# One transformer kernel with its instruction order redrawn: new prices in the planner, and engines chosen by it

## The chip, the cores and the metric

The kernel runs on one core of one Trainium2 chip. The metric is the device time of one execution in microseconds, here the median of three runs. The core has five engines that run side by side: TensorE (PE, with its weight loads as PEld), VectorE (DVE), ScalarE (ACT), GpSimd (POOL) and SyncE (SP), which in this kernel only issues DMAs.

## The reference

Two layers of a diffusion backbone in float32, on 512 latent tokens and 256 context tokens of 1024 features. Each layer is a token mixer and a squared-ReLU MLP, both on normalised input that a vector `c` shifts, scales and gates (adaLN).

```python
for i in range(DEPTH):                     # DEPTH = 2
    mod_lat = (silu_c @ ada_w[i] + ada_b[i])[:, None, :]
    mod_ctx = (silu_cc @ ada_w[i] + ada_b[i])[None, None, :]
    u_lat = modulate(rms_norm(h_lat, g_mix[i]), sh1, sc1)
    u_ctx = modulate(rms_norm(h_ctx, g_mix[i]), csh1, csc1)
    # layer 0: 16 heads, 2-D neighbourhood attention with a bias table, plus all context keys
    # layer 1: 16 query heads on 4 key heads, window of 128, rotary embedding, a sink logit
    h_lat = h_lat + ga1 * y_lat
    h_lat = h_lat + ga2 * squared_relu_mlp(modulate(rms_norm(h_lat, g_mlp[i]), sh2, sc2), mlp_w1[i], mlp_w2[i])
    # layer 0 does the same for the context rows; layer 1 does not need them
```

## The kernel before

Large products are made exact enough by splitting: each operand becomes a rounded part and a rest (`split`, line 581: a copy on ACT, a subtraction on DVE or POOL), and three products stand for one. Activations are kept as features by tokens in `FA`, split operands in `RA`, both cut by hand into rings of slots.

In order of time the stages are: the start (modulation of the first layer, first QKV, `ada01`, `mods01`, `mod0`); the first attention (`qkv0`, `attn0`, from about 90 us); output projection and entry of the first MLP (about 400 to 500 us); the first MLP in 16 chunks with the second layer's modulation made on ACT and POOL beside it (`ada`, to 1045 us); keys, values and queries of the second layer (`kv1`); the second attention (`Head1`, to about 1290 us); the second MLP on latent tokens only.

The order of the instructions isn't the order of the code. Calls on engines only record steps. `Plan` knows which step needs which, gives each step a cost (`cost`, line 206), and plays the program through its own model of the five engines (`forward`, line 276): at each time the engine that is free first takes the ready step with the lowest rank. `search` repeats this 40 times with other ranks, keeps the shortest, and the steps are then issued engine by engine in that order (line 432, to which the profile puts nearly all instructions). SP's queue is a part of the plan, so loads are reordered too. The engine of a step is fixed in the code: `v`, `s`, `g` stand for DVE, ACT, POOL.

Names that matter below: `load` (line 559) issues a DMA from SP; `bias_tables` (line 780) copies 32 pieces of the relative bias into a table in DRAM, from which every head of the first attention reads (`attn0`, line 933); `ada_ring`, `raw` and `w0` are the rings that loads of the start wait for; `Stats.step` sums squares for a norm; `dup_mult` (line 816) scales queries and keys by their norms; `evac_pt` (line 919) and `merge` (line 925) bring attention results out of PSUM; in `attn0` and `Head1.front` the probabilities are multiplied by the reciprocal of their sum, on DVE for most blocks and on POOL for one in four; `Stream.fill` loads and splits weights, with POOL as the subtracting engine around the entries of the MLPs (`stream.eng = g`) and DVE in their bodies.

Of the kernel before, what the change touches and what calls it, by code (L numbers as in the profile page):

```python
# [10 lines left out]
F32 = mybir.dt.float32  # L11
# [8 lines left out]
L = 512  # L20
# [68 lines left out]
class Step:  # L89


    def __init__(self, eng):
        self.eng, self.calls, self.reads, self.writes = eng, [], [], []
        self.epoch, self.deps, self.succ = None, set(), []
        self.occ = self.dur = 0.0
        self.mode, self.port, self.bytes = "R", False, 0.0

# [18 lines left out]
class Plan:  # L116
    LANES = {"tensor": "PE", "vector": "DVE", "scalar": "ACT", "gpsimd": "POOL", "sync": "SP"}
    ALL = ("PE", "DVE", "ACT", "POOL", "SP")
    WINDOW = 3413.3

# [35 lines left out]
    def add(self, step):  # L156
# [4 lines left out]
        for x, write in [(x, False) for x in step.reads] + [(x, True) for x in step.writes]:  # L161
# [9 lines left out]
            for k in self.cells(x):  # L171
# [3 lines left out]
                if write:  # L175
                    d.update(r)
                elif kind == "PSUM":

                    d.update(j for j in r if self.steps[j].eng != step.eng)
# [9 lines left out]
        d.discard(i)  # L189
        self.cost(step)  # L190
# [15 lines left out]
    def cost(self, x):  # L206
        if x.eng == "PE":
# [9 lines left out]
            if kind == "t":  # L217
                x.occ, x.dur = 109.0, 272.0
# [22 lines left out]
        else:  # L241
            f, args, kw = x.calls[0]
            data = [(y, *width(y)) for y in x.reads]
            n = max(width(y)[0] for y in x.reads + x.writes)
            here = [(y, m) for y, _, m in data if self.space(y) == "SBUF" and m > 8]
            psum = any(self.space(y) == "PSUM" for y in x.reads)
            if x.eng == "ACT":
                two = f == "activation" and len(data) > 1
                x.dur = (165 + 0.81 * n if psum else 195 + 0.83 * n) + (95 if two else 0) + (90 if kw.get("accum_out") is not None else 0)
                if n <= 8:  # L250
                    x.dur = 297.0 if two else 205.0
                x.occ = x.dur - 105
            elif x.eng == "DVE":
                x.dur = 148 + 1.045 * n
                if len(data) > 2:
                    x.dur += 62
                if n <= 16:
                    x.dur = 157.0
                elif f == "tensor_scalar" and not psum:
                    x.dur = 225 + 0.51 * n  # L260
                x.occ = x.dur - 82 + (82 if kw.get("accum_out") is not None else 0)
                x.port = f not in ("tensor_reduce", "reciprocal", "memset") and not psum and (len(here) > 1 or f in ("tensor_scalar", "tensor_copy") or n <= 8)
            else:
                wide = any(m < k for _, k, m in data)
                x.dur = 470 + 2.33 * n if f == "tensor_scalar" else 80 + 0.8 * n if f in ("memset", "affine_select") else 170 + (1.75 if wide else 2.2) * n
                x.occ = x.dur - 45
                x.port = f not in ("memset", "affine_select")

    LAG = {"PE": 54.0, "POOL": 80.0, "SP": 60.0, "DVE": 35.0, "ACT": 35.0}
# [6 lines left out]
    def forward(self, rank):  # L276

        L = self.steps
        n = len(L)
        wait = [len(x.deps) for x in L]  # L280
# [5 lines left out]
        for x in L:  # L286
            if not x.deps:
                heapq.heappush(coming[x.eng], (0.0, rank[x.i], x.i))
        for _ in range(n):
            t, e = min((max(free[e], min(([free[e]] if now[e] else []) + ([coming[e][0][0]] if coming[e] else []))), k, e) for k, e in enumerate(self.ALL) if now[e] or coming[e])[::2]  # L290
            while coming[e] and coming[e][0][0] <= t + 1e-6:
                _, k, i = heapq.heappop(coming[e])
                heapq.heappush(now[e], (k, i))
            k, i = heapq.heappop(now[e])
            x = L[i]
            if e == "PE" and x.mode != mode and now[e]:

                later = [(k, i)]
                while now[e] and now[e][0][0] < k + 250:
                    y = heapq.heappop(now[e])  # L300
                    if L[y[1]].mode == mode:
# [11 lines left out]
            if e == "PE":  # L313
# [5 lines left out]
                pre = 0.0 if x.mode == mode else 95.0 if mode == "R" else 100.0  # L319
# [12 lines left out]
            elif e == "SP":  # L332
                free[e] = t + x.occ
                dma = max(t + 1500, dma) + x.bytes
                end[i] = dma + 800
            else:
                hold = max(0.0, port - t) if x.port else 0.0
                free[e] = t + hold + x.occ
# [1457 lines left out]
```

## Time and profile before

| | us |
|---|---|
| median of three runs | 1660.36 (1658.4 to 1661.73) |
| profiled execution | 1661.9 |
| its span, first to last instruction | 1660.1 |
| PE busy in it | 1601.2 |
| mean granted clock of TensorE | 0.992 |

The profile is of one execution. Busy time of an engine is the time in which it has at least one instruction under way; products overlap in PE, so a busy PE need not be a well-fed one. A stage is a stretch of the span. The granted clock is the share of full speed that TensorE was given; it has two levels, 1.2 and 2.4 GHz. A wait belongs to what ended last before the waiting instruction could start.

### The profile page before, as it was taken

What the parts mean: (1) busy time and instruction counts of PE and PEld (TensorE: products, weight loads), DVE (VectorE), ACT (ScalarE), POOL (GpSimd) and SP (SyncE); (2) the same over time, 40 slices, a digit from 0 to 9 for tenths busy, and PEclk for the clock granted to TensorE, in tenths of its full rate; (3) what the DMA queues carried; (4) which work ended last, traced back from release to release, by engine and by line L of the source; (5) the groups of instructions that cost most, each with busy time, mean ns of one, the idle gap of its engine ahead of it and who ended that gap; (6) DMA issues with size and microseconds to landing.
All of it is one profiled execution on the core that took longest, in us unless ns stands there. A gap on an engine that the chain in (4) does not pass through costs nothing.

```text
span 1660.1 us, 25159 instructions
## 1 busy us (share of the span) xinstructions
PE 1601.2 (96%) x9554; PEld 1357.5 (82%) x9554; DVE 1136.5 (68%) x2178; ACT 808.7 (49%) x1668; POOL 553.9 (33%) x371
## 2 busy tenths in 40 slices
PE   4999999999989999999999999999999899999999
PEld 3878888987778888888888888797767888888887
DVE  4787666778458656675666666899996766655654
ACT  4587666778435334344352433658874522332320
POOL 1121111122247419485682652475631400000000
PEclk9999999999999999999999999999999899999999
DMA  9723443114314334334342332010114232233301
GB/s 295 213 74 102 134 150 121 47 42 126 103 63 128 97 101 132 103 114 127 115 140 76 115 106 73 32 58 14 46 45 146 89 102 90 89 101 102 102 26 52
DMA packets 63802, 165.63 MB, mean 100 GB/s; under 512 B 6848, under 2 KB 24640, under 8 KB 63552
## 3 DMA queue, kind: packets, MB, share of 16 engines
q1 hardware_dynamic: 63680, 164.02, 31.2%
q8 instruction: 75, 1.23, 0.3%
q14 instruction: 47, 0.39, 0.1%
HBM read 159.79 MB, written 7.34 MB: 101 GB/s over the span
## 4 chain that ended last, share of the span: by engine, by line
PE 80%; DVE 8%; ACT 5%; issue 3%; DMA 3%; POOL 1%; SPq 0%; POOLq 0%; DVEq 0%; ACTq 0%
PE pq L432 80%; DVE FA L432 3%; DVE RA L432 2%; ACT RA L432 2%; DVE smalls L432 1%; DMA FA<-in_ada_w_dram 1%; ACT FA L432 1%; ACT R L432 1%; DMA FA<-in_wqkv_dram 1%; POOL FA L432 0%; DVE R L432 0%; ACT smalls L432 0%; DMA R<-in_ada_w_dram 0%; SPq L432 0%; DMA FA<-in_wo_dram 0%
## 5 line engine op out<-in xcount | busy, mean ns | idle before, releaser
L432 PE MATMUL pq<-RA 128*128 128x512 f32 (+3 forms) x6784 | 1268.5, 342 | 13.1 <-DVE RA L432 5.4
L432 PEld LDWEIGHTS pq<-RA 128*128 128x128 f32 x6784 | 1083.1, 190 | 166.8 <-issue 16.6
L432 ACT CAST RA<-FA 128x1024 fp32r<-128x1024 f32 (+3 forms) x283 | 224.9, 812 | 370.7 <-PE pq L432 256.5
L432 DVE TENSOR_TENSOR RA<-FA,RA 128x1024 fp32r<-128x1024 f32 (+3 forms) x249 | 297.5, 1209 | 113.6 <-ACT RA L432 109.9
L432 DVE SCALAR_TENSOR_TENSOR FA<-pq,mods,FA 128x512 f32<-128x512 f32 (+1 forms) x413 | 266.0, 662 | 138.6 <-PE pq L432 137.4
L432 POOL TENSOR_TENSOR R<-R,FA 128x1024 f32<-128x1024 f32 x84 | 218.2, 2628 | 6.7 <-ACT FA L432 4.6
L432 POOL TENSOR_TENSOR FA<-FA,smalls 128x512 f32<-128x512 f32 (+1 forms) x108 | 95.9, 892 | 322.5 <-DVE smalls L432 250.4
L432 PE MATMUL pq<-RA,R 128*128 128x512 f32 (+1 forms) x870 | 177.6, 353 | 3.4 <-DVE RA L432 3.4
L432 PEld LDWEIGHTS pq<-RA,R 128*128 128x128 f32 x870 | 144.4, 191 | 27.6 <-DVE RA L432 3.8
L432 POOL TENSOR_SCALAR FA<-FA,s 128x1024 f32<-128x1024 f32 x24 | 77.5, 3230 | 180.8 <-DMA FA<-in_ada_w_dram 166.0
L432 PE MATMUL pq<-ident,FA 128*128 128x128 f32 x802 | 124.1, 276 | 9.4 <-DVE FA L432 2.5
L432 PEld LDWEIGHTS pq<-ident,FA 128*128 128x128 f32 x802 | 92.0, 140 | 30.4 <-issue 9.4
L432 POOL TENSOR_TENSOR FA<-FA 128x256 f32<-128x256 f32 (+2 forms) x97 | 75.2, 791 | 120.2 <-ACT FA L432 109.4
L432 POOL TENSOR_TENSOR RA<-FA,RA 128x1024 fp32r<-128x1024 f32 (+2 forms) x34 | 72.4, 2140 | 128.5 <-ACT RA L432 96.4
L432 ACT COPY R<-pq 128x512 f32<-128x512 f32 (+3 forms) x200 | 89.6, 477 | 37.6 <-PE pq L432 36.4
L432 ACT ACTIVATE FA<-FA,smalls 128x512 f32<-128x512 f32 (+1 forms) x120 | 89.1, 743 | 25.4 <-DVE smalls L432 25.0
L432 ACT COPY FA<-pq 128x256 f32<-128x256 f32 (+4 forms) x130 | 56.1, 432 | 87.5 <-PE pq L432 80.1
L432 ACT ACTIVATE FA<-FA,s 128x1024 f32<-128x1024 f32 x60 | 69.1, 1151 | 60.1 <-POOL FA L432 50.8
L432 DVE SCALAR_TENSOR_TENSOR FA<-pq,FA 128x512 f32<-128x512 f32 (+1 forms) x96 | 57.1, 596 | 53.5 <-ACT FA L432 53.4
L432 ACT ACTIVATE FA<-pq 128x512 f32<-128x512 f32 (+1 forms) x96 | 49.9, 522 | 73.0 <-PE pq L432 71.9
L432 ACT ACTIVATE FA<-FA 128x256 f32<-128x256 f32 (+1 forms) x131 | 59.0, 457 | 49.5 <-DVE FA L432 38.3
L432 PE MATMUL pq<-R 128*64 128x512 f32 (+2 forms) x448 | 78.9, 463 | 0.0
(77 smaller groups left out, 979.1 us busy)
## 6 DMA issues: line engine op xcount, KB each, us to landing
FA<-in_w_dram SPq DMA_DIRECT2D x128, 512.0 KB, 3.5
FA<-in_ada_w_dram SPq DMA_DIRECT2D x80, 512.0 KB, 3.9
FA<-in_wqkv_dram SPq DMA_DIRECT2D x32, 384.0 KB, 3.7
FA<-in_wo_dram SPq DMA_DIRECT2D x16, 512.0 KB, 3.5
FA<-in_ada_w_dram SPq DMA_DIRECT2D x20, 256.0 KB, 5.9
FA<-in_wq_dram SPq DMA_DIRECT2D x8, 512.0 KB, 3.6
R<-in_ada_w_dram SPq DMA_DIRECT2D x12, 256.0 KB, 6.3
FA<-in_xT_dram SPq DMA_DIRECT2D x4, 512.0 KB, 7.7
```

The costliest lines, as they stand in the source:

```text
L432: tc.keep_in_program_order(getattr(e, f)(*map(real, args), **{k: real(x) for k, x in kw.items()}))
```

## The change

Three things change, all of them in how the plan is drawn.

First, the planner's prices. Each instruction on DVE, ACT and POOL is planned 40 ns longer than its price (`SPARE`). PE's turning between kinds of product has a table (`TURN`) in place of one number, DMAs are planned to land 2000 instead of 800 ns after their bytes, POOL's answer takes 110 instead of 80 ns, a change of the partitions that an engine starts at costs it a drain, and DVE and POOL hold each other off where both need the port that they share.

Second, steps with several forms. `gv` is "POOL or DVE", `sv` "ACT or DVE", and `scaled` "POOL, DVE or ACT", each with POOL or ACT first in the list. Such a step waits in the queues of all its engines. The first engine of the list gives it up when another would end it earlier by more than the step's slack and 50 ns; another engine takes it early only when its slack is small. Weight splits, sums of squares, norm scalings, rope products, PSUM copies, and the scaling of probabilities become such steps.

Third, loads made through `load` before the first attention are issued in program order (`strict`). That puts the bias tables' copies behind the loads of the first modulation and QKV weights, among the loads of the next QKV weights.

```diff
+    SPARE = 40.0
...
+            forms = x.forms or {x.eng: x.calls[0]}
+            for e, c in forms.items():
+                occ, dur, port = self.vector_cost(x, e, *c)
+                x.costs[e] = occ + self.SPARE, dur + self.SPARE, port
+            x.occ, x.dur, x.port = x.costs[x.eng]
...
+    TURN = {("t", "R"): -81.0, ("R", 64): 92.0, ("R", 32): 90.0, ("t", 64): 93.0, ("t", 32): 93.0,
+            (64, "R"): 62.0, (64, "t"): 62.0, (32, "R"): 137.0, (32, "t"): 137.0, (32, 64): 112.0, (64, 32): 112.0, (64, 64): -38.0, (32, 32): 22.0}
+    DRAIN = {"DVE": 113.0, "ACT": 127.0, "POOL": 0.0}
-    LAG = {"PE": 54.0, "POOL": 80.0, "SP": 60.0, "DVE": 35.0, "ACT": 35.0}
+    LAG = {"PE": 54.0, "POOL": 110.0, "SP": 60.0, "DVE": 35.0, "ACT": 35.0}
...
+            if e == "POOL" and owner == "DVE" and port > t + 150 and L[now[e][0][1]].costs[e][2]:
+                free[e] = port - 65
+                continue
...
+            if x.forms:
+                own, slack = x.costs[e][1], k - t
+                if e == x.eng:
+                    best = min(max(free[o], t) + c[1] for o, c in x.costs.items())
+                    if free_choice and t + own > best + max(50.0, slack):
+                        dropped.add(i)
+                        continue
+                elif i not in dropped:
+                    main = max(free[x.eng], t) + x.costs[x.eng][1]
+                    if not free_choice or slack > main - t + 200 or main <= t + own:
+                        heapq.heappush(coming[e], (t + 300, k, i))
+                        continue
+                gone[i] = True
+                eng[i] = e
...
-                pre = 0.0 if x.mode == mode else 95.0 if mode == "R" else 100.0
+                pre = self.TURN.get((mode, x.mode), 0.0)
...
-                end[i] = dma + 800
+                end[i] = dma + 2000
...
-                hold = max(0.0, port - t) if x.port else 0.0
+                hold = max(0.0, port - t - 138) if shared and owner != e else 0.0
+                if low[e] != x.low or not x.low and e == "DVE":
+                    hold += self.DRAIN[e]
...
+    gv, sv = Engine("gpsimd", "vector"), Engine("scalar", "vector")
+    def scaled(out, x, by, flat):
+        y = Step("POOL")
+        y.forms = {"POOL": ("tensor_tensor", (), dict(out=out, in0=x, in1=by, op=ALU.mult)),
+                   "DVE": ("tensor_scalar", (), dict(out=out, in0=x, scalar1=flat, scalar2=None, op0=ALU.mult)),
+                   "ACT": ("activation", (out, x, AF.Copy), dict(scale=flat))}
+        y.calls, y.reads, y.writes = [y.forms["POOL"]], [x, by], [out]
+        plan.add(y)
...
-    load = sy.dma_start
+    strict = [True]
+    def load(out, in_):
+        x = sy.dma_start(out, in_)
+        if strict[0]:
+            if strict[1:]:
+                x.after = strict.pop().i
+                x.deps.add(x.after)
+            strict.append(x)
...
     def split(H_, L_, x, eng=None):
         s.copy(H_, x)
-        (eng or v).tensor_tensor(out=L_, in0=x, in1=H_.bitcast(F32), op=ALU.subtract)
+        gv.tensor_tensor(out=L_, in0=x, in1=H_.bitcast(F32), op=ALU.subtract)
...
-                g.tensor_tensor(out=acc[0], in0=acc[0], in1=tmp, op=ALU.add)
+                gv.tensor_tensor(out=acc[0], in0=acc[0], in1=tmp, op=ALU.add)
...
                 s.activation(q, h, AF.Square)
-                eng.tensor_tensor(out=R, in0=R, in1=q, op=ALU.add)
+                gv.tensor_tensor(out=R, in0=R, in1=q, op=ALU.add)
...
-        (v.tensor_copy if eng is v else s.copy)(pt[:, 0 : hi - lo], ps[:, lo:hi])
+        sv.copy(pt[:, 0 : hi - lo], ps[:, lo:hi])
...
-            if t == 0:
-                g.tensor_tensor(out=P, in0=P, in1=sm.broadcast_to([128, 512]), op=ALU.mult)
-            else:
-                v.tensor_scalar(out=P, in0=P, scalar1=sm, scalar2=None, op0=ALU.mult)
+            scaled(P, P, sm.broadcast_to([128, 512]), sm)
...
     weave((qk, 6), (bias_tables(), 16))
+    strict[0] = False
...
-            v.tensor_tensor(out=hL, in0=q, in1=hH.bitcast(F32), op=ALU.subtract)
+            gv.tensor_tensor(out=hL, in0=q, in1=hH.bitcast(F32), op=ALU.subtract)
...
-            g.tensor_tensor(out=h4(y), in0=h4(x), in1=rope[:, 2 * e, t].unsqueeze(1).broadcast_to([128, 4, DH]), op=ALU.mult)
+            gv.tensor_tensor(out=h4(y), in0=h4(x), in1=rope[:, 2 * e, t].unsqueeze(1).broadcast_to([128, 4, DH]), op=ALU.mult)
```

Copies out of PSUM in `merge`, the fronts of the projections and the values become `sv`; the remaining products of `roped` and `dup_mult` become `gv`; the scalings of `Head1.front` become `scaled` in the same way as those shown.

## Rows read from the trace of the kernel before

**Rows 1.** The page, part 1: busy us, share of span, instructions.

```profile
PE 1601.2 (96%) x9554; PEld 1357.5 (82%) x9554; DVE 1136.5 (68%) x2178; ACT 808.7 (49%) x1668; POOL 553.9 (33%) x371
```

**Rows 2.** Stages: length, busy PE, PEld, DVE, ACT, POOL; granted clock, DMA share, GB/s.

```profile
20.00:100.00 80.00, 70.03 (x585) 60.15 (x577) 58.06 (x148) 46.17 (x125) 17.03 (x22) 0.96 0.66 200
100.00:470.00 370.00, 362.89 (x2433) 310.72 (x2432) 247.77 (x719) 249.64 (x677) 74.96 (x82) 1.00 0.31 99
470.00:501.00 31.00, 24.62 (x133) 21.02 (x132) 20.88 (x30) 14.98 (x25) 16.18 (x8) 0.83 0.22 68
501.00:1045.00 544.00, 544.00 (x3140) 472.95 (x3140) 369.18 (x487) 217.86 (x299) 312.49 (x126) 1.00 0.35 110
1045.00:1095.00 50.00, 46.15 (x278) 39.26 (x277) 44.88 (x85) 29.59 (x64) 25.66 (x31) 1.00 0.09 27
1095.00:1300.00 205.00, 199.28 (x1390) 158.51 (x1390) 178.35 (x432) 142.29 (x333) 89.31 (x91) 0.99 0.19 61
1300.00:1320.00 20.00, 16.59 (x109) 15.73 (x108) 13.03 (x20) 9.69 (x17) 10.30 (x5) 0.83 0.34 106
1320.00:1660.00 340.00, 336.75 (x1489) 278.32 (x1487) 198.62 (x245) 90.87 (x118) 7.31 (x3) 1.00 0.26 84
```

**Rows 3.** Chain of waits, shares by line: 501 to 1045, 1095 to 1310 us.

```profile
by line: PE pq L432 100.0%
...
by line: PE pq L432 67.8%; DVE FA L432 14.5%; issue 4.1%; DVE R L432 3.0%; ACT FA L432 3.0%; DVE RA L432 2.6%; DVE smalls L432 1.7%; ACT R L432 1.7%; ACT RA L432 1.5%; ACT smalls L432 0.4%; DVEq L432 0.0%; ACTq L432 0.0%
```

**Rows 4.** Timeline of SP's queue and PE: start, us, instructions, wait before.

```profile
8.59 0.34 SPq L432 DMA_DIRECT2D cst<-in_cst_dram  x1
...
20.27 5.17 SPq L432 DMA_DIRECT2D bias_e<-in_rpb_dram  x7
...
57.32 1.01 SPq L432 DMA_DIRECT2D FA<-in_wqkv_dram  x2
...
19.06 1.94 PE L432 MATMUL pq<-FA,s 128*32 128x128 f32 x32 [19.06 <-DVE s L432]
...
57.56 10.50 PE L432 MATMUL pq<-RA 128*128 128x384 f32 x59
...
91.56 3.29 PE L432 MATMUL pq<-RA 128*128 128x256 f32 x20 [0.42 <-DVE smalls L432]
```

**Rows 5.** Timeline, all engines, entry of the first MLP.

```profile
478.99 10.56 POOL L432 TENSOR_TENSOR RA<-FA,RA 128x1024 fp32r<-128x1024 f32 x3 [6.45 <-ACT RA L432]
...
479.64 0.74 DVE L432 SCALAR_TENSOR_TENSOR FA<-FA,amod 128x512 f32<-128x512 f32 x1
...
479.91 8.35 PE L432 MATMUL pq<-RA 128*128 128x512 f32 x36
...
484.83 2.48 DVE L432 SCALAR_TENSOR_TENSOR FA<-FA,amod 128x512 f32<-128x512 f32 x1
...
494.64 1.22 PE L432 MATMUL pq<-FA,ones 128*128 128x256 f32 x2 [6.38 <-POOL FA L432]
...
495.30 5.25 PE L432 MATMUL pq<-RA 128*128 128x512 f32 x11
```

**Rows 6.** Groups: busy us, mean ns, idle; second attention (three), first, whole span.

```profile
L432 DVE TENSOR_SCALAR FA<-FA,smalls 128x640 f32<-128x640 f32 x24 | 20.1, 865 | 0.0
...
L432 DVE TENSOR_SCALAR FA<-FA,smalls 128x512 f32<-128x512 f32 x16 | 12.5, 780 | 0.1
...
L432 POOL TENSOR_TENSOR FA<-FA,smalls 128x512 f32<-128x512 f32 x28 | 31.3, 1124 | 44.6 <-DVE smalls L432 31.6 <-ACT R L432 7.5 <-ACT FA L432 5.4
...
L432 DVE TENSOR_SCALAR FA<-FA,smalls 128x512 f32<-128x512 f32 x39 | 18.7, 492 | 0.1
...
L432 POOL TENSOR_TENSOR RA<-FA,RA 128x1024 fp32r<-128x1024 f32 x19 | 50.1, 2646 | 60.0 <-ACT RA L432 36.1 <-PE pq L432 21.4 <-DVE RA L432 2.5
```

**Rows 7.** Timeline, entry of the second MLP.

```profile
1308.20 2.56 DVE L432 SCALAR_TENSOR_TENSOR RA<-FA,mods,RA 128x256 fp32r<-128x256 f32 x1
...
1310.81 0.80 PE L432 MATMUL pq<-RA,R 128*128 128x256 f32 x2 [3.39 <-DVE RA L432]
```

More of the change, by code (lines that the diff above doesn't have):

```diff
@@ L177, in add @@
                 elif kind == "PSUM":
[L179 removed]
+                    d.update(j for j in r if self.steps[j].forms or step.forms or self.steps[j].eng != step.eng)
                 spots.append((k, write))
@@ L189, in add @@
         d.discard(i)
+        if step.eng not in ("PE", "SP"):
+            step.low = all(geometry(x)[1] == 0 for x in step.reads + step.writes)
         self.cost(step)
@@ L241, in cost @@
         else:
[L242 to L262, printed above, removed]
-            else:
[L264 to L267, printed above, removed]
@@ L269, with vector_cost @@
-    LAG = {"PE": 54.0, "POOL": 80.0, "SP": 60.0, "DVE": 35.0, "ACT": 35.0}
+            forms = x.forms or {x.eng: x.calls[0]}
[3 more added lines that the diff above has]
+            x.occ, x.dur, x.port = x.costs[x.eng]
+    def vector_cost(self, x, eng, f, args, kw):
+        port = False
+        data = [(y, *width(y)) for y in x.reads]
+        n = max(width(y)[0] for y in x.reads + x.writes)
+        here = [(y, m) for y, _, m in data if self.space(y) == "SBUF" and m > 8]
+        psum = any(self.space(y) == "PSUM" for y in x.reads)
+        if eng == "ACT":
+            two = f == "activation" and len(data) > 1
+            dur = (165 + 0.81 * n if psum else 195 + 0.83 * n) + (95 if two else 0) + (90 if kw.get("accum_out") is not None else 0)
+            if n <= 8:
+                dur = 297.0 if two else 205.0
+            occ = dur - 105
+        elif eng == "DVE":
+            dur = 148 + 1.045 * n
+            if len(data) > 2:
+                dur += 62
+            if n <= 16:
+                dur = 157.0
+            elif f == "tensor_scalar" and not psum:
+                dur = 225 + 0.51 * n
+            occ = dur - 82
+            port = f not in ("tensor_reduce", "reciprocal", "memset") and not psum and (len(here) > 1 or f in ("tensor_scalar", "tensor_copy") or n <= 8)
+        else:
+            wide = any(m < k for _, k, m in data)
+            dur = 470 + 2.33 * n if f == "tensor_scalar" else 80 + 0.8 * n if f in ("memset", "affine_select") else 170 + (1.75 if wide else 2.2) * n
+            occ = dur - 45
+            port = f not in ("memset", "affine_select")
+        return occ, dur, port
@@ L334, in forward @@
                 dma = max(t + 1500, dma) + x.bytes
[L335 removed]
+                end[i] = dma + 2000
             else:
[L337 to L341 removed]
+                occ, dur, shared = x.costs[e]
+                hold = max(0.0, port - t - 138) if shared and owner != e else 0.0
+                if low[e] != x.low or not x.low and e == "DVE":
+                    hold += self.DRAIN[e]
+                low[e] = x.low
+                free[e] = t + hold + occ
+                end[i] = t + hold + dur
+                if shared:
+                    port, owner = end[i], e
             for j in x.succ:
[L343 to L344 removed]
+                to = L[j].eng if not L[j].forms else "DVE"
+                r = start[i] + 1 if e == to == "PE" or L[j].after == i else end[i] + self.lag(e, to)
                 if r > ready[j]:
@@ L392, in search @@
         for k in range(rounds):
-            start, end, order, last = self.forward(rank)
+            start, end, order, last = self.forward(rank, k > 0)
             if best is None or last < best[0]:
```

78 lines of the change are left out of this document (44 added, 34 removed).

## The prediction

> **What bounds the kernel now.** I read the page's busy table first: TensorE is busy 96% of the span, and no other engine is over 68% [rows 1]. A share over the whole span hides where the slack is, so the second view is the busy time by stage [rows 2]. The reader should look at two columns there: the stretch's length against PE's busy time. In the two MLP bodies, 501 to 1045 and 1320 to 1660 us, PE is busy 544.00 of 544.00 and 336.75 of 340.00; the chain of waits, the third view, says the same, 100.0% PE for the first [rows 3]. Nothing that moves vector work can shorten these 884 us. The rest is idle time at the edges: 9.97 us between 20 and 100 us (80.00 - 70.03), 7.11 us in the first attention (100 to 470), 6.38 us at the entry of the first MLP (470 to 501), 3.85 us at the start of the second layer (1045 to 1095), 5.72 us in the second attention (1095 to 1300) and 3.41 us at the entry of the second MLP (1300 to 1320). With the 19.06 us before the first product [rows 4], that is some 55 us, and PE's idle time is a lower bound of what is lost: "busy" runs on while a product waits half-fed. The chain from 1095 to 1310 us shows it: only 67.8% of it is PE, 69 of 215 us are DVE, ACT and issue [rows 3]. The timelines of the worst places, last, tell what ended each wait.
>
> **The change, part by part.** It adds and removes no work. The same arithmetic is issued, by another engine here and there, in another order; 40 ns of spare at each vector instruction is a number in the planner and costs nothing on the chip. So each part is worth what it takes out of the waits just listed, and can cost whatever new waits the new order makes. Six terms:
>
> **1, the start.** The ring of first loads is now issued in program order, so the 32 copies of the bias tables go behind all the weights of the first modulation. Now seven of them take 5.17 us of SP's queue [rows 4], 0.74 each, so 32 hold it for some 24 us, between 20.27 us and the last two loads of the first QKV weights at 57.32 us. The constants too are issued only at 8.59 us, and the first product waits for what is made of them until 19.06 us. Gain: at most 9.97 us of idle time plus the 8.6 us by which the constants could at most be issued earlier, 18.6 us; loss: up to 8 us, below, if the tables become the last to arrive. I take 6 us, nearer to the idle row than to the sum, since the weights still have to come at the rate that the DMA engines give (they are 66% busy from 20 to 100 us [rows 2]).
>
> **2, first attention.** 7.11 us idle in 370 us. The planner gets new prices for PE's turning between kinds of product, and evacuations may go to DVE or ACT as they are free. No row isolates a turn, so the bounds are 3 us lost and 7 us gained; I take 3 us gained, the middle of the idle time.
>
> **3, entry of the first MLP.** Here POOL runs three 1024-wide weight splits in one piece, 10.56 us; DVE's operation from 484.83 us takes 2.48 us beside it, against 0.74 us for its like at 479.64; and the sums for the context's norm, queued on POOL behind the splits, release PE only at 494.64 us, 6.38 us late [rows 5]. After that PE runs at the lower granted clock (0.83 in the stage, of levels 1.2 and 2.4 GHz): eleven products in 5.25 us against 36 in 8.35, so 11 x (0.477 - 0.232) = 2.7 us more. Splits and sums may now each go to DVE, and the planner holds one engine back while the other has the port. Bounds 0 and 9 us, I take 6: both causes are named in the diff, and what is late next is the modulation on DVE and ACT, which ends within about 3 us of the sums.
>
> **4, start of the second layer.** 3.85 us idle; POOL's rope products may go to DVE, but DVE is 44.88 of 50 us busy there [rows 2], so it can take little. 0 to 3.9 us, I take 2.
>
> **5, second attention.** DVE is busy 178.35 of 205 us, POOL 89.31, ACT 142.29 [rows 2]. 24 normalisations of 128x640 take DVE 865 ns and 16 of 128x512 take 780 ns, while the 128x512 form takes 492 ns in the first attention, where POOL does less [rows 6]. The stretch alone is at least 16 x 0.288 = 4.6 us, and for the 640-wide form, scaled from 492 (x 640/512 = 615), 24 x 0.250 = 6.0 us. These can now go to ACT or POOL, as can evacuations to whichever of ACT and DVE is free. Gain at most 5.7 us of idle time plus the 10.6 us of stretch, 16 us; at worst a POOL product of 1124 ns [rows 6] stands where 492 ns stood. I take 8 us, half.
> The pages speak against this term. The Trainium skill ("Perfetto Trace Analysis", section Optimizing Scalar/DVE Operations) says that moving work between GpSimd and VectorE might not help, as they share a port to SBUF. If that were all, term 5 would be 0 and the time below 1648 instead of 1643.
>
> **6, entry of the second MLP.** The picture of term 3 again: a DVE operation of 2.56 us, for 256 columns, while POOL splits weights, and PE idle 3.39 us until DVE is done [rows 7]; the granted clock is 0.83 there [rows 2], which by term 3's ratio (0.477 to 0.232) is worth another 2 to 3 us. 0 to 6 us, I take 4.
>
> **The MLP bodies, at nothing.** What hides any engine choice there is PE. Were all 64 splits of the first MLP to land on POOL at 2.646 us [rows 6], that is 169 us on top of 312.49: 482 of 544 us, still under the stage. In the second it is 7 + 169 of 340. If that cover went, a split that is late costs PE one wait of at most its own 2.6 us.
>
> Sum: 6 + 3 + 6 + 2 + 8 + 4 = 29 us, with bounds of 60 us gained and 11 us lost on terms 1 and 2 alone. But the order now in use was drawn by a search of the same kind, and it left all these waits; a new one will miss some and make others. I keep 60%: 17 us. The profiled execution took 1661.9 us (span 1660.1 and 1.8 around it), so 1645; the median of the runs is 1.5 us below it: **1643 us**.
>
> **The rivals.**
> *A, POOL by default (slower).* In each "either" step POOL stands first in the list, DVE takes it only when little slack is left by the plan. A product that DVE did in 0.49 us then sits on POOL for 1.12 [rows 6], and each time POOL holds the port a DVE operation that is due takes 2.48 instead of 0.74 us [rows 5]. If eight more of these 1.74 us blocks land where PE waits, in the second attention and at the MLP entries, they cost 13.9 us; terms 3 to 6 are then lost, terms 1 and 2 give 0.6 x 9 = 5.4: +8.5, 1669 us. It decides from about ten blocks on, where they eat the whole 17 us. For it: POOL has room in every stage [rows 2]. Against: the planner now prices the port and POOL's answer higher.
> The Trainium skill ("SBUF — State Buffer", section Who interferes with whom) calls the pair an exclusive lock, the second engine fully blocked until the first is done. The 2.48 us row agrees.
> *B, no change.* The search may pick a round in which hardly any engine changes, or trade old waits for new: 1660 us. For it: PE is 96% busy. Against: the waits of terms 3 and 6 are single and have a cause that the change touches.
> *C, all 29 us.* The real prices fit and the six waits go: 1631 us.
> *D, the tables last.* Loads in strict order wait for each other's buffers: most bias copies can only follow the next QKV weights, which wait for buffers that the first products free, at 68 us (57.56 + 10.50). 24 us of issues from there end at 92, later than the 91.56 us of the first scores [rows 4], and the tables must still be read back; at an estimated 5 us for that (seven copies' issue time, rounded) the start loses 5 us instead of gaining 6. The other terms give 0.6 x 23 = 14: 1661.9 - 9 - 1.5, 1651 us. It decides where the copies end after 87 us.
>
> **How the numbers follow.** About 0.2%, 3.3 us, is what a measurement of this kernel can tell from no change. Forecast (1634 to 1650) 0.45, C 0.15, D 0.10, B 0.13, A 0.17. Faster: 0.70; same 0.13; slower 0.17. The range leaves out half of C's better end and most of A's: 1625 to 1664 us.
>
> **What would show it.** Term 1: the bias copies issued after the first QKV weights, first scores before 88 us. Terms 3 and 6: no PE wait over 3 us at the two MLP entries and a clock near 1.00 there. Term 5: the chain of the second attention over 75% PE, and the DVE forms near 500 and 600 ns. A: POOL's busy time well over 554 us, with more DVE operations of 2 us and longer. D: first scores after 95 us. Wrong altogether if an MLP body takes longer than it does now.

## The result and the profile after

The changed kernel takes 1647.8 us (median of 4 runs, 1647.1 to 1648.0) against 1660.7 us (1658.4 to 1661.7) for the kernel before on the same chip: a ratio of 0.9914, 95% interval 0.9888 to 0.994. It is faster by 12.8 us, 0.8%. Its profiled span is 1645.3 us against 1660.1.

The page of after, part 1 (busy time, share, instructions) and the head of part 4 (chain):

```profile
PE 1599.2 (97%) x9554; PEld 1354.5 (82%) x9554; DVE 789.2 (48%) x1712; ACT 823.2 (50%) x1684; POOL 1146.6 (70%) x821
PE 91%; DVE 4%; ACT 2%; DMA 1%; issue 1%; POOL 1%; SPq 0%; ACTq 0%; DVEq 0%; POOLq 0%
```

Beside [rows 1]: DVE has 466 instructions less (2178 to 1712), POOL 450 more (371 to 821), ACT 16 more. POOL's busy time has doubled. So the free choice of an engine has in practice been a move from DVE to POOL: 454 of the 1105 steps that may choose went that way, 4 the other way, and 16 went from DVE to ACT.

To see where the 15 us of span are, I cut both traces not at fixed times but at the same work: the first softmax instruction, the 64th (last) of the first attention, the first relu of the first MLP, its 64th (last), the first relu of the second MLP, and PE's end. Each row of the windows view is then one stage; the columns are those of [rows 2] (length, busy PE, PEld, DVE, ACT, POOL, granted clock, DMA share, GB/s). Before:

```profile
0.00:90.80 90.80, 62.19 (x533) 53.20 (x534) 56.95 (x143) 46.19 (x116) 14.51 (x24) 0.96 0.78 244
90.80:412.70 321.90, 315.39 (x2178) 272.92 (x2178) 229.71 (x707) 235.32 (x658) 64.06 (x75) 1.00 0.32 99
412.70:499.70 87.00, 79.60 (x446) 65.64 (x445) 45.10 (x65) 35.85 (x64) 30.30 (x18) 0.95 0.25 79
499.70:1002.20 502.50, 502.50 (x2913) 437.38 (x2912) 335.62 (x433) 202.20 (x270) 295.24 (x108) 1.00 0.36 113
1002.20:1319.60 317.40, 304.42 (x2002) 249.76 (x2001) 270.47 (x589) 197.82 (x445) 142.32 (x143) 0.98 0.19 61
1319.60:1656.70 337.10, 337.10 (x1490) 278.63 (x1489) 198.14 (x244) 91.27 (x119) 7.51 (x3) 1.00 0.26 83
```

After:

```profile
0.00:81.40 81.40, 61.80 (x555) 51.62 (x556) 47.93 (x114) 45.52 (x114) 34.67 (x44) 0.95 0.87 280
81.40:398.70 317.30, 314.72 (x2158) 274.98 (x2157) 196.46 (x591) 239.74 (x663) 184.40 (x201) 1.00 0.32 99
398.70:481.00 82.30, 78.87 (x449) 64.44 (x447) 32.99 (x50) 34.53 (x62) 45.53 (x29) 1.00 0.22 71
481.00:982.40 501.40, 501.17 (x2904) 436.26 (x2905) 175.30 (x313) 203.39 (x271) 470.50 (x230) 1.00 0.36 113
982.40:1305.60 323.20, 306.35 (x2009) 249.05 (x2008) 219.44 (x485) 208.93 (x461) 238.96 (x233) 0.98 0.19 62
1305.60:1641.90 336.30, 336.30 (x1487) 278.11 (x1485) 116.60 (x160) 91.14 (x119) 172.49 (x87) 1.00 0.26 83
```

Stage by stage the change brings 9.4 us at the start, 4.6 in the first attention, 4.7 at the entry of the first MLP, 1.1 in its body, **loses 5.8 in the second layer up to its MLP**, and brings 0.8 in the last body: 14.8 in all. The fifth row is the one to look at: DVE has 51 us less to do there, and the stage is longer.

That stage can be cut once more, at the first and the last softmax instruction of the second attention. Before, then after:

```profile
1002.20:1097.70 95.50, 91.65 (x531) 78.50 (x530) 81.79 (x146) 47.84 (x103) 45.53 (x53) 1.00 0.17 56
1097.70:1248.30 150.60, 147.05 (x1060) 113.96 (x1061) 140.57 (x371) 117.66 (x286) 81.74 (x85) 1.00 0.12 36
1248.30:1319.60 71.30, 65.72 (x415) 57.30 (x412) 48.11 (x75) 32.31 (x58) 15.05 (x7) 0.93 0.38 122
```

```profile
982.40:1071.30 88.90, 87.18 (x492) 74.16 (x490) 68.91 (x123) 47.70 (x98) 53.78 (x62) 1.00 0.18 62
1071.30:1230.40 159.10, 151.19 (x1080) 116.61 (x1080) 113.86 (x311) 126.63 (x303) 140.57 (x145) 1.00 0.12 38
1230.40:1305.60 75.20, 67.98 (x440) 58.28 (x439) 36.68 (x52) 34.60 (x63) 44.61 (x28) 0.93 0.35 116
```

The order moved some products from one of these parts to the next, so PE's idle time (length less busy) is the figure to compare. It fell from 3.9 to 1.7 us ahead of the attention, rose from 3.6 to 7.9 us in the attention, and from 5.6 to 7.2 us behind it: 3.9 us more in all. The other 1.9 us of the 5.8 are longer busy time for the same products.

The groups of instructions between 1045 and 1300 us of both traces (busy us, mean ns | idle before) show what DVE and POOL do instead. First the two commonest small forms before, then the same after, with the normalisations that POOL has now:

```profile
L432 DVE SCALAR_TENSOR_TENSOR smalls<-smalls 128x4 f32<-128x4 f32 x44 | 15.3, 355 | 0.3
L432 DVE TENSOR_TENSOR smalls<-smalls 128x4 f32<-128x4 f32 x38 | 12.1, 320 | 2.6 <-ACT smalls L432 2.4
```

```profile
L489 DVE SCALAR_TENSOR_TENSOR smalls<-smalls 128x4 f32<-128x4 f32 x40 | 22.3, 559 | 0.4
L489 DVE TENSOR_TENSOR smalls<-smalls 128x4 f32<-128x4 f32 x36 | 18.4, 511 | 3.4 <-ACT smalls L489 3.1
L489 POOL TENSOR_TENSOR FA<-FA,smalls 128x512 f32<-128x512 f32 x53 | 54.8, 1040 | 12.9 <-DVE smalls L489 10.6 <-ACT FA L489 2.2
L489 POOL TENSOR_TENSOR FA<-FA,smalls 128x640 f32<-128x640 f32 x24 | 29.9, 1253 | 1.4 <-DVE smalls L489 1.4
```

The normalisations of [rows 6] have left DVE altogether, and a DVE instruction of these two forms on four columns takes 511 to 559 ns in the mean where it took 320 to 355.

The sharpest place is the entry of the second MLP, to be held against [rows 7]. Timeline of DVE, POOL and PE (start, us, instruction, wait before it):

```profile
1280.96 2.32 DVE L489 SCALAR_TENSOR_TENSOR RA<-FA,mods,RA 128x256 fp32r<-128x256 f32 x1 [0.19 <-ACT RA L489]
1285.72 2.61 DVE L489 TENSOR_TENSOR FA<-FA 128x256 f32<-128x256 f32 x1
1288.25 2.60 DVE L489 SCALAR_TENSOR_TENSOR RA<-FA,mods,RA 128x256 fp32r<-128x256 f32 x1
...
1280.60 4.92 POOL L489 TENSOR_TENSOR RA<-FA,RA 128x1024 fp32r<-128x1024 f32 x2
1285.69 2.35 POOL L489 TENSOR_TENSOR RA<-FA,RA 128x1024 fp32r<-128x1024 f32 x1 [0.18 <-ACT RA L489]
1287.99 2.57 POOL L489 TENSOR_TENSOR R<-FA,R 128x1024 fp32r<-128x1024 f32 x1
...
1283.33 0.62 PE L489 MATMUL pq<-RA,R 128*128 128x256 f32 x3 [1.85 <-DVE RA L489]
1288.38 1.22 PE L489 MATMUL pq<-FA,ones 128*128 128x256 f32 x2 [4.07 <-DVE FA L489]
1290.90 1.43 PE L489 MATMUL pq<-RA,R 128*128 128x256 f32 x5 [1.30 <-DVE RA L489]
```

POOL splits four weights of 1024 columns here; each of the three DVE instructions of 256 columns ends just behind a split (1285.72 + 2.61 = 1288.33, the split at 1288.04; 1288.25 + 2.60 = 1290.85, the split at 1290.56), and PE waits 1.85 + 4.07 + 1.30 = 7.2 us for DVE, where the kernel before waited 3.39. These four splits were POOL's in the kernel before too; the new order set them against these instructions, not the choice of engine: e1 below, the new order with the old engines, has the same 7.2 us of idle time behind the second attention.

### The profile page after: what moved, and what is told of

It is laid out like the page before. It is cut to its first block, busy times and chain, and to the rows that moved or that the text cites. A ratio compares the mean times of both kernels' runs of the same rounds, so it can differ in the third digit from the quotient of the medians.

```text
span 1645.3 us, 25439 instructions
## 1 busy us (share of the span) xinstructions
PE 1599.2 (97%) x9554; PEld 1354.5 (82%) x9554; DVE 789.2 (48%) x1712; ACT 823.2 (50%) x1684; POOL 1146.6 (70%) x821
## 3 DMA queue, kind: packets, MB, share of 16 engines
q8 instruction: 75, 1.23, 0.3%
## 4 chain that ended last, share of the span: by engine, by line
PE 91%; DVE 4%; ACT 2%; DMA 1%; issue 1%; POOL 1%; SPq 0%; ACTq 0%; DVEq 0%; POOLq 0%
PE pq L489 91%; DVE FA L489 2%; DVE RA L489 1%; ACT FA L489 1%; ACT RA L489 1%; POOL RA L489 0%; DVE smalls L489 0%; ACT R L489 0%; DMA FA<-in_xT_dram 0%; DMA bias_e<-in_rpb_dram 0%; DMA FA<-in_ada_w_dram 0%; POOL FA L489 0%; SPq L489 0%; DMA FA<-in_cT_dram 0%; DVE R L489 0%
## 5 line engine op out<-in xcount | busy, mean ns | idle before, releaser
L489 POOL TENSOR_TENSOR RA<-FA,RA 128x1024 fp32r<-128x1024 f32 (+3 forms) x282 | 503.3, 1801 | 251.4 <-ACT RA L489 216.5
L489 POOL TENSOR_TENSOR FA<-FA,smalls 128x512 f32<-128x512 f32 (+3 forms) x254 | 212.7, 860 | 140.5 <-DVE smalls L489 131.3
L489 POOL TENSOR_TENSOR R<-R,FA 128x1024 f32<-128x1024 f32 x84 | 201.7, 2433 | 3.4 <-ACT FA L489 3.4
L489 PE MATMUL pq<-ident,FA 128*128 128x128 f32 x802 | 130.6, 276 | 3.2 <-ACT R L489 2.0
L489 ACT COPY R<-pq 128x512 f32<-128x512 f32 (+4 forms) x216 | 97.7, 480 | 47.3 <-PE pq L489 45.8
L489 PEld LDWEIGHTS pq<-ident,FA 128*128 128x128 f32 x802 | 95.3, 140 | 23.6 <-issue 7.7
L489 POOL TENSOR_TENSOR FA<-FA 128x256 f32<-128x256 f32 (+2 forms) x121 | 88.1, 745 | 20.9 <-ACT FA L489 17.7
L489 POOL TENSOR_TENSOR R<-FA,R 128x1024 fp32r<-128x1024 f32 x25 | 60.8, 2435 | 41.4 <-ACT R L489 41.4
L489 DVE SCALAR_TENSOR_TENSOR RA<-pq,cst,RA 64x128 fp32r<-64x128 f32 (+2 forms) x152 | 58.0, 383 | 50.5 <-ACT RA L489 48.5
```

Of the source, the lines that this page charges most:

```text
L489: tc.keep_in_program_order(getattr(e, f)(*map(real, args), **{k: real(x) for k, x in kw.items()}))
```

## The experiments

Two kinds of run have to be kept apart. Where the order of the steps is *frozen* (e1, e2, e5, e6, e9, e10), only the edit differs. Where the planner *draws the order anew* (e3, e4, e7, e8, e11, e12), the edit and another order come together; e7, e11 and e12 show how much another order can move. Runs of one group share a chip, and the kernel before was timed again on each: 1659.8 us beside e1 to e4, 1661.7 beside e5 to e8, 1659.9 beside e9 to e11, 1660.0 beside e12. The ratios are to these.

**e1, e2: the order and the engines, one without the other.** The engine of each step that may choose is a letter of the string `FIXED`, the order a packed list of step numbers, `ORDER`; the two come from different kernels. Cut to the lines that matter:

```diff
+        if step.forms:
+            e = {"D": "DVE", "A": "ACT", "P": "POOL"}.get(FIXED[self.flexible])
+            self.flexible += 1
+            if e:
+                step.eng, step.calls, step.forms = e, [step.forms[e]], {}
...
-        for step in plan.search(ROUNDS):
+        for step in (plan.steps[i] for i in np.frombuffer(zlib.decompress(base64.b85decode(ORDER)), np.int16)):
```

> The changed kernel's order of steps, kept step by step, with the engines of the kernel before (471 of the 1105 steps with a choice go back, 454 of them from POOL to DVE, 16 from ACT to DVE as copies). Theory 'order' (the gain is the loads' order and the new prices; the engines are a wash or a loss): 1640 to 1650 us, first scores near 81 us as in the changed kernel. Theory 'engines' (the gain is that DVE is unloaded): 1655 us or more, since DVE is back at some 1130 us busy.

> The order of the kernel before, kept step by step, with the engines that the changed kernel chose. Theory 'order': 1660 us or more, first scores at 91 us as before, and the POOL splits late for products that were planned behind DVE ones. Theory 'engines': 1645 to 1652 us.

The new order with the old engines took 1668.3 us (ratio 1.0048, 1.0031 to 1.0065), the old order with the new engines 1732.8 us (1.0438, 1.042 to 1.0455). Neither half is an improvement: each is slower than the kernel before, by 8.6 and 73 us, and together they are faster by 12.8. Both theories missed: 'order' had 1640 to 1650 for e1, 'engines' 1645 to 1652 for e2. In the body of the first MLP the loss of e2 is 1032.3 - 516.0 = 516.3 us against 502.5. An order is drawn for its engines; the gain cannot be split between the two.

**e3, e4: a part left out, the order drawn anew.**

```diff
-    strict = [True]
+    strict = [False]
```

> The changed kernel without the program order among the first loads; planned anew. Theory 'order of the loads': the 9 us that the first scores came earlier (90.8 to 81.4 us) are lost, 1654 to 1658 us, bias copies from about 20 us on again. Rival (the earlier start comes from the new prices of DMA landings and turns): 1646 to 1650 us and first scores still before 85 us.

In e4 every step that may choose keeps the engine it had before (`FIXED` as above, the order from the search).

> The changed kernel with every engine as in the kernel before and the rest (prices, spare, loads in order) kept; planned anew. Theory 'order': 1638 to 1646 us, faster than the changed kernel, since the second layer no longer waits for POOL (from the first relu of the first MLP to that of the second 820 us or less against 825). Theory 'engines': 1655 to 1660 us, DVE busy again over 85% in the second attention.

Without the strict order of loads: 1652.5 us (0.9951, 0.9934 to 0.9967). The first softmax comes at 95.3 us, 13.9 later than with it and 4.5 later than before, but the median is only 4.7 us over the changed kernel's, between the ranges of the two theories; the execution that was profiled, the slowest of four, is 10.1 us over. So between a quarter and two thirds of what is lost at the start comes back later. Without the choice of engines: 1656.3 us (0.9982, 0.9973 to 0.9992), in the range of theory 'engines'. Its start is as good (first softmax at 78.7), its first MLP's body takes 507.0 us instead of 501.4 and its second layer 329.7 instead of 323.2 (317.4 in the kernel before). So that stage grew with the old engines too: PE is idle for 9.2 us of the second attention there, 3.6 in the kernel before:

```profile
1083.10:1244.60 161.50, 152.32 (x1053) 117.16 (x1052) 143.65 (x374) 118.95 (x288) 83.49 (x84) 0.97 0.10 34
```

**e8: the strict loads alone,** put into the kernel before, everything drawn anew by the old planner.

> The kernel before with one part of the change alone: the first loads in program order; planned anew with the old prices and engines. Theory 'order of the loads by itself': first scores near 81 us instead of 90.8, 1649 to 1653 us. Rival (strict order pays only with the new price of a DMA's landing): first scores after 87 us, 1656 us or more.

1654.6 us (0.9947, 0.9929 to 0.9964). First softmax at 81.9 us, as in the changed kernel, first relu of the MLP at 488.7, of the second MLP at 1313.1: of the 8.9 us of lead at the first softmax, 6.5 are left at the second MLP. The start is as theory 'order of the loads by itself' had it; the time is between the ranges of the two theories. This is the part of the change that I would call understood: the six draws with the loads in program order have their first softmax between 78.7 and 83.3 us, the two without at 90.8 and 95.3. The copies of the tables no longer begin at 20.27 us with seven in one piece [rows 4] but at 35.23 us, among the QKV weights. The constants are issued at 2.59 us instead of 8.59 [rows 4], and the first modulation product (`FA,s`) starts at 14.58 us (13.45 in e8) instead of 19.06. The constants are not enough by themselves: e3 issues them at 3.18 us and the copies from 18.88 us on, and its first modulation product starts at 19.29 us. The queue of SP and the first products in the changed kernel:

```profile
2.59 0.65 SPq L489 DMA_DIRECT2D cst<-in_cst_dram  x1
...
35.23 0.65 SPq L489 DMA_DIRECT2D bias_i<-in_rpb_i_dram  x1
35.99 0.54 SPq L489 DMA_DIRECT2D bias_e<-in_rpb_dram  x1
36.79 0.37 SPq L489 DMA_DIRECT2D FA<-in_wqkv_dram  x1
...
73.16 0.54 SPq L489 DMA_DIRECT2D bias_e<-in_rpb_dram  x1
...
12.58 2.07 PE L489 MATMUL pq<-FA,ones 128*128 128x512 f32 x2 [12.58 <-POOL FA L489]
14.58 2.64 PE L489 MATMUL pq<-FA,s 128*32 128x128 f32 x64
```

**e5: the second layer in its old order,** behind the first layer of the changed kernel; engines and order of each layer are those of the kernel that it comes from.

> The changed kernel's order and engines up to the end of the first MLP, then the order and engines of the kernel before for everything from the second layer's keys on, kept step by step. Theory 'the second layer lost what the first gained in part' (19.8 us ahead at the end of the first MLP, 14.0 us at the first relu of the second): 1640 to 1644 us. Rival (the second layer's length hangs on what the first leaves behind in buffers and queues, not on its own order): 1646 us or more.

1653.7 us (0.9942, 0.9921 to 0.9963). The second layer up to its MLP takes 327.6 us: longer than in either kernel (317.4 and 323.2). That is the rival's forecast. Behind this beginning the old order is no gain; that the new order of the second layer is bad as such was not shown this way.

**e6: four splits from POOL to DVE.** The changed kernel with its order frozen; the four weight splits at the entry of the second MLP that the timeline above shows go to DVE, in POOL's place in the order (the steps 11097, 11100, 11131 and 11162). They were POOL's in the kernel before as well, so this does not undo a part of the change. One line of `FIXED` differs:

```diff
-    "PPPPAAAAAAPPPPAAPAAAAPPPPAAAAAAAAPPPPPPPPPPPPPPPPPPPDPPPPPPPPPPPPPPPPPPPPPPPPPPPPPPPPPPPPPPPPPPPPPPPPPPPPPPPPPPPPPPPPPPP"
+    "PPPPAAAAAAPPPPAAPAAAAPPPPAAAAAAAAPPPPPPPPPPPPPPPPPPPDPPPDDPDPDPPPPPPPPPPPPPPPPPPPPPPPPPPPPPPPPPPPPPPPPPPPPPPPPPPPPPPPPPPP"
```

> The changed kernel's order and engines kept step by step, with one thing moved: the four 1024-wide weight splits around the entry of the second MLP go from POOL to DVE. Theory 'port' (DVE's modulation and sums take 2.3 to 2.6 us there because POOL's splits hold the port): the three waits of PE there (1.85, 4.07 and 1.30 us) shrink to under 1 us each and the clock stays up, 1639 to 1643 us. Rival (in DVE's queue the splits wait for ACT's rounding of late weights, and the modulation waits behind them): no gain or slower, 1647 us or more.

1640.6 us (0.9863, 0.9839 to 0.9888), 7.2 us less than the changed kernel, from four instructions, as theory 'port' had it. In the traces the part behind the second attention takes 68.5 us instead of 75.2, with 1.6 us of idle time instead of 7.2. The same instructions of DVE and the same wait of PE:

```profile
1282.42 0.48 DVE L497 SCALAR_TENSOR_TENSOR RA<-FA,mods,RA 128x256 fp32r<-128x256 f32 x1 [0.19 <-ACT RA L497]
1283.44 1.22 DVE L497 TENSOR_TENSOR RA<-FA,RA 128x1024 fp32r<-128x1024 f32 x1
1284.97 0.42 DVE L497 TENSOR_TENSOR FA<-FA 128x256 f32<-128x256 f32 x1
...
1285.44 1.13 PE L497 MATMUL pq<-FA,ones 128*128 128x256 f32 x2 [1.47 <-DVE FA L497]
```

2.32 us became 0.48, 2.61 became 0.42, and 4.07 us of waiting 1.47 (under 1 was forecast); the other two waits are gone. A split costs DVE 1.22 us where it cost POOL 2.35 to 2.57. The Trainium skill ("SBUF — State Buffer", section Who interferes with whom) calls the port that the two share an exclusive lock. These rows agree: the DVE instruction was not slowed in proportion, it ended 0.29 us behind POOL's, whenever it had begun.

**e9, e10: more splits.** e9 moves five further splits in the same frozen order (three ahead of the first MLP, two at the start of the second layer), e10 28 in all: beside those nine, 19 of 1024 columns that POOL does in the second attention and around the entry of the second MLP. The five of e9, too, were POOL's in the kernel before. The line of `FIXED` for the three:

```diff
-    "AAAPPAAAAAAPPPPPPAAPPAAAAPPAAAAAPPPPPPPPPPPPPPPPPPPPAAAAAAAPPPPAAAAAAAPPPPPPPPPPPPPPPPPPDDPPPPPPPPPPPPPPPPPPPPPPPPPPPPPP"
+    "AAAPPAAAAAAPPPPPPAAPPAAAAPPAAAAAPPPPPPPPPPPPPPPPPPPPAAAAAAAPPPPAAAAAAAPPPPPPPPPPPPPPPPPPDDPPDDPPDPPPPPPPPPPPPPPPPPPPPPPP"
```

> Keeps the step order of the changed kernel and the four weight splits that the run before had put on VectorE (1640.6 us), and puts five more 1024-wide weight splits of GpSimd on VectorE at the place that GpSimd had for them in the order: the three ahead of the first MLP (GpSimd 464.2 to 472.6 us, beside VectorE instructions of 2.5 to 2.9 us) and two at the start of the second layer (beside 128x4 instructions of 3.85 us at 1058.4 and 2.30 us at 1075.5). Theory (VectorE waits out each wide split of GpSimd, and TensorE waits behind VectorE): the TensorE waits of 2.76 us at 470.6 and 2.5 us at 1075.8 shrink to under 0.8 us, the VectorE instructions there take 0.5 to 0.8 us, and the median falls by 3 to 5 us, to 1636 to 1638. Rival (the order was drawn up around GpSimd there, and five more splits of 1.2 us on VectorE delay it by as much as they free): within 1 us of 1640.6. Rival (the gain at the second MLP was particular to that place): slower than 1641.

> As the run before with nine splits moved, and all the other 1024-wide weight splits that GpSimd does between 1050 and 1290 us of the plan, 28 moved in all. It tells whether moving wide work to VectorE helps wherever VectorE has waiters, or only ahead of a stage's start. Theory A (each one blocks VectorE by up to 2.4 us and a split costs VectorE 1.2 us, so each move gains): the second layer up to the first instruction of its MLP is 2 to 6 us shorter than with nine moved, median 1631 to 1636. Theory B (in the middle of the attention GpSimd's splits fall where VectorE has time to spare, and VectorE in order now waits for ScalarE's rounding copy ahead of each split): no change or up to 5 us slower than with nine moved, 1637 to 1643.

e9: **1636.8 us** (0.986, 0.9843 to 0.9876), the fastest version to use, 23 us under the kernel before and 11 under the changed one. The entry of the first MLP in the changed kernel, and in e9:

```profile
466.27 2.51 DVE L489 SCALAR_TENSOR_TENSOR RA<-FA,mods,RA 128x512 fp32r<-128x512 f32 x1
468.70 2.88 DVE L489 SCALAR_TENSOR_TENSOR FA<-FA,amod 128x512 f32<-128x512 f32 x1
471.51 2.57 DVE L489 TENSOR_TENSOR FA<-FA 128x256 f32<-128x256 f32 x1
465.37 8.43 POOL L489 TENSOR_TENSOR RA<-FA,RA 128x1024 fp32r<-128x1024 f32 x3
```

```profile
465.41 0.73 DVE L497 SCALAR_TENSOR_TENSOR RA<-FA,mods,RA 128x512 fp32r<-128x512 f32 x1
466.07 0.74 DVE L497 SCALAR_TENSOR_TENSOR FA<-FA,amod 128x512 f32<-128x512 f32 x1
466.73 0.41 DVE L497 TENSOR_TENSOR FA<-FA 128x256 f32<-128x256 f32 x1
469.45 1.21 DVE L497 TENSOR_TENSOR RA<-FA,RA 128x1024 fp32r<-128x1024 f32 x1
```

Three instructions of 7.96 us became 1.88, and the stage and the second layer, cut as above:

```profile
397.80:476.30 78.50, 78.25 (x448) 64.51 (x446) 29.12 (x52) 34.41 (x61) 37.22 (x26) 1.00 0.21 74
977.80:1294.00 316.20, 304.40 (x2009) 247.00 (x2008) 213.18 (x490) 208.73 (x461) 225.94 (x227) 1.00 0.18 60
```

82.3 us became 78.5 with PE idle for 0.25 us, and 323.2 became 316.2. Of these 7.0 us the four splits of e6 give all: the part behind the second attention takes 68.1 us, the part ahead of it 88.8 us as in the changed kernel (88.9; 91.2 in e6, where nothing was moved there), so the two splits at the start of the second layer brought nothing. The median is as the theory had it, 3.8 us under e6; by the ratios, each on its own chip, e6 and e9 are almost equal (0.9863 and 0.986), so the 3.8 us rest on the stage in the traces (82.3 us in the changed kernel, 82.8 in e6, 78.5 in e9). e10 took 1637.3 us (0.986, 0.9846 to 0.9875): from the first softmax to the first relu of the second MLP 1213.0 us against 1212.7 in e9. Theory B's time held: the other 19 moves neither gain nor lose. Its reason, that DVE has time there that nobody waits for, fits but was not tested by itself. What counted here is whether PE waits behind the blocked instruction, not how many are blocked.

**e7, e11, e12: the spare room.** 0, 50 and 2 ns in place of 40, all drawn anew.

```diff
-    SPARE = 40.0
+    SPARE = 0.0
```

> The changed kernel with no spare at the vector instructions, all else kept; planned anew. Theory 'spare' (a plan with room survives the drift of real durations): 1652 to 1660 us. Rival (the spare is only another draw of the order): within 4 us of the changed kernel's 1647.8, on either side.

> The changed kernel with 50 ns instead of 40 ns of spare room at each vector instruction of the plan; everything else, engines too, is drawn up anew. It tells whether 7.6 us between no spare (1655.4) and 40 ns (1647.8) are the spare room's or those of another draw. If the spare itself is worth it, 10 ns more changes little: 1645.5 to 1650. If a redrawn order is mostly a draw, this one lands anywhere between 1645 and 1656, and off 1647.8 by 3 us or more.

> The changed kernel with 2 ns of spare room instead of 40 ns at each vector instruction of the plan: next to none, as in the run with no spare (1655.4 us), but another draw of the order. If spare room itself is what brought 1655.4 down to 1647.8, this one is as slow as without it: 1653 to 1657. If 7.6 us are what one draw differs from the next, it may land anywhere between 1643 and 1656, and a time under 1650 would show that the spare room isn't needed for it.

0 ns: 1655.4 us (0.9973, 0.9952 to 0.9993). 50 ns: 1643.9 us (0.9901, 0.9885 to 0.9917). 2 ns: 1631.5 us (0.9824, 0.9808 to 0.984). Two nanoseconds bring 24 us, three times what 40 bring (7.6). e11 and e12 fell below every range that was forecast for them. So the spare room as such has no price that these runs could show: what they show is the spread of drawn orders. Read alone, e7 would have put 7.6 us down to the spare room. The losses of e3 and e4, 4.7 and 8.5 us, are of the size of that spread, so neither is shown to be a part's own price; and beyond the start, the same holds for the change's gain.

In the order of e12 eight steps stand ahead of a step whose result they use (five normalisations ahead of their reciprocal, among others), in that of e11 one; so these two times measure orders and are no versions to use, and the 24 us are an upper end: between the two sound draws, 0 and 40 ns, it is 7.6. But the eight steps run between 1048 and 1232 us, and the order of e12 is ahead before them: the last relu of the first MLP comes at 978.1 us, at 988.4 in the profiled execution of e7 (which is 4.7 us over e7's median) and at 982.4 in the changed kernel. The planner can draw such an order because an engine that puts a step off keeps its old free time, and its next step may then begin before its input is ready (read from `forward`, not tested). What e12 would take with the eight steps in their place was not tried. Its page:

```profile
PE 1596.8 (98%) x9554; PEld 1355.6 (83%) x9554; DVE 1190.7 (73%) x2425; ACT 815.4 (50%) x1628; POOL 174.7 (11%) x164
```

This draw went the opposite way from the changed kernel's: nearly everything to DVE, POOL at 11%. Its second layer up to the MLP takes 312.7 us, the shortest of all, with 268.3 us on DVE. It gains most over the changed kernel at the entry of the first MLP (76.4 us; e9 78.5), ahead of all early steps, and behind the second attention (64.0 us; e9 68.1), the two places where seven of e9's nine splits lie; e12 has all nine on DVE. In the second layer the early steps cannot be told apart from that in this one run, so that fewer locks are the cause of 1631.5 us is argued, not shown; the shown part is e6 and e9.

## Why the prediction was right, and where it was not

1643 us was forecast, with 1625 to 1664 around it; 1647.8 came. Sign and size hold, but the sum holds by terms that cancel, and that is luck.

- **Term 1, the start: mechanism right, undersized.** 6 us forecast, 9.4 measured; e8 alone has 8.9. The first modulation product comes 4.5 us earlier (19.06 to 14.58); the product that is now first, at 12.58, is another one, which does not wait for the constants. The details of the test failed, though: the tables' copies do not stand behind the QKV weights but between them, from 35.2 to 73.2 us. Rival D fell with that: it had the copies wait until 68 us.
- **Term 2, the first attention.** 3 forecast, 4.6 measured; PE's idle time fell from 6.5 (321.90 - 315.39) to 2.6 us. It goes with the prices: e4, with the old engines, has this stage at 317.0 us, e8, with the old prices, at 320.9. Which price does it stays open.
- **Term 3, the entry of the first MLP.** 6 forecast, 4.7 measured. The test passed (no wait over 3 us; the granted clock of the stage went from 0.95 to 1.00), yet the cause that I named was still there: the splits did not leave POOL, and three of them held DVE up for 6 us. e9 took that away and the stage lost another 3.8 us.
- **Terms 4 to 6, the second layer: the step that failed.** 14 forecast, -5.8 measured. Term 4 holds: PE's idle time ahead of the attention fell by 2.1 us, 2 forecast. Terms 5 and 6 failed: 8 forecast and 4.4 us more idle time in the attention, 4 forecast and 1.6 us more behind it. Two errors. First, term 5 counted 10.6 us of stretched DVE instructions as time that PE would get back. [rows 3] had 67.8% PE in the chain, and I read the rest as loss; but the windows cut by work show PE idle for 13.0 of 317.4 us before, 3.6 of them in the attention. Beyond idle time only slower products could give anything back, and for the same products PE was busy between 301.2 us (e12) and 319.4 us (e2). DVE lost 51 us of work and PE gained nothing by it. Second, I took the sign of "may go to either engine" from what would be good, not from what stands first in the list. The stretched forms were to go back near 500 and 600 ns on DVE; instead they went to POOL at 1040 and 1253. That this move cost the time is not shown: e4, which leaves them on DVE, has 9.2 us of idle time in the attention. Why the attention got worse, with either set of engines, stays open: it may be the prices or the draw (5.6 us idle in e3, 5.0 in e8 with the old prices). For term 6 e6 shows the cause: four splits stayed on POOL beside the instructions that PE waits for.
- **Term 5 at nothing.** The prediction gave 1648 us for that case, and 1647.8 came, by chance: the second layer did not stay as it was but lost 5.8 us, and the start gave 3.4 more than forecast.
- **The tests of that stage.** The chain between 1095 and 1290 us is now 78.1% PE, over the 75% that I had asked for, in a stage that got longer. A share of a chain says nothing of the chain's length; the test was a wrong one. Term 6's test did its work: PE waits 4.07 us at the entry, and the clock is 0.61 between 1283 and 1296 us.
- **The MLP bodies, at nothing.** 1.1 and 0.8 us. POOL is 470.5 of 501.4 us busy in the first, close to the 482 that I had worked out as the worst, and PE still covers it.
- **Rival A, POOL by default.** Half right. POOL's 1147 us and the engines are as it says. DVE instructions of 2 us and over fell from 41 to 13, but only because 32 of the 41 were weight and activation splits of DVE itself, which are now POOL's; the others rose from 9 to 13, as A said. The new prices do not keep the two engines apart: e4 has them with the old engines, and 43 such instructions. A needed 17 us of blocks to decide. The blocks that e6 and e9 take away, 7.2 and 3.8 us, are not among those that A meant: all nine splits were on POOL in the kernel before, were free to go to DVE, and stayed. The two runs price what the change left undone, not what it did.
- **The discount.** 29 us at 60% was 17, and 14.8 came, but not since every term gave 60%: the first three gave 18.7 of 15, the other three -5.8 of 14. A forecast that is right by its sum is no proof of its steps.

## What to carry to other kernels

Before pricing a stretched instruction on a side engine, cut the trace at the same work and take the bound engine's idle time in that stage as the first measure of what can come back; a chain's share of other engines is not that. In a kernel like this one, look for wide GpSimd instructions beside a VectorE instruction that TensorE waits for: four splits in the right place were worth about half of this change, three others 3.8 us, and 21 further ones nothing. A planner that is free to move such steps need not do so. And where an order is drawn by a search, measure some draws before crediting a part of the change with a few microseconds: here two sound ones differ by 7.6, and all of them by up to 24.

## What was not expected of the hardware

- The block went with the split and not with the blocked instruction's size: 256 columns took 2.3 to 2.6 us beside a split of 1024 columns instead of 0.42 to 0.48, and at 1075.94 us of after one on four columns took 2.02 us, where its like in e9 took 0.48 with the split beside it moved to DVE. It works the other way too: a POOL instruction on 256 columns took 2.66 us at 462.75 us while DVE ran, against 0.74 us at 456.70.
- Instructions too small to matter show how often the two engines meet. Between 1045 and 1300 us POOL is busy for 38 us in e12, 115 in the kernel before and 211 in the changed one; the two forms on four columns take DVE 161 and 163, 320 and 355, 511 and 559 ns in the mean.
- A split of 1024 columns takes 2.35 to 2.86 us on POOL in the changed kernel at the nine places of e9, and 1.21 to 1.23 us on DVE there (1.40 once), about half.
- In the changed kernel the granted clock falls to its lower level (0.50, of levels 1.2 and 2.4 GHz) while PE waits: just before 1286 us, inside the wait of 4.07 us, after a wait of 1.85 us and 0.62 us of products. It is back at 1296 us, 7.6 us after PE went on. With a wait of 1.47 us in its place e6 has the lower level from about 1286 to 1289 us; e9, with a wait of 1.47 us behind the same instructions, keeps 1.00. So the length of this one wait does not settle it.
